# A two-layer decoder trunk in one kernel: one more seven-product pair in four feed-forward blocks, residual additions by accumulating DMAs, and bank sums ordered ahead of a weight subtraction

## The chip, the cores and the metric

The kernel runs on one core of one Trainium2 chip. The metric is the device time of one execution in microseconds (us); the median of several executions is compared. A change of less than 0.2% (5.1 us) is treated as no change.

## The reference

An input x of 256 rows by 2048 features (float32) passes through two layers. Layer 0 mixes with an mLSTM and a Mamba-2 head group between one input and one output projection, layer 1 with block-sparse attention. Each layer ends in a SwiGLU feed-forward stage of width 5632, which is where most of the change lies:

```python
def swiglu(x, w_gate, w_up, w_down):
    return (jax.nn.silu(x @ w_gate) * (x @ w_up)) @ w_down

for layer in range(DEPTH):
    xn = rms_norm(x, norm_mix[layer])
    x = x + (mixer_mlstm_ssd(xn, ...) if layer % 2 == 0 else mixer_moba(xn, ...))
    x = x + swiglu(rms_norm(x, norm_ffn[layer]), *ffn_params[layer])
return rms_norm(x, final_norm)
```

## The kernel before

Every float32 product is made of three matmuls: each operand is split into a high part (rounded to the fast format fp32r) and a low part (the rest), and high x high, high x low and low x high are added up (`add`, L487 to L489). Activations are split once and kept as blocks of four row tiles (class `KT`). Weights are streamed: `weights` loads 256 rows of two strips of 512 columns into the tile `raw` (two DMAs of 512 KB on the SP queue), ScalarE casts them to `wh` (L453) and VectorE subtracts to get `wl` (L455).

`block` computes the product of 256 rows by two strips over `nk` row tiles of the weights. It takes the row tiles in pairs, each pair in one of two ways, given by a plan string such as PSPSPSPP. A "P" pair is done as eight block products of two row tiles: 24 matmuls into the four accumulators `F` (called `acc_f`). An "S" pair is done by Winograd's form of Strassen's scheme with seven block products: 21 matmuls into `F` and four more accumulators `E` (called `acc_e`). For it VectorE forms sums of weight quarters (`sums`: L462, L463, L465) and sums of activations (`activation_sums`, held in a tile called `skh` with three buffers or `skx`). `pairs` says which row-tile pairs are done the S way; `ahead` holds functions that are called at a given place of the plan, here to make activation sums (`sums_of`).

All eight banks of the accumulator memory are in use: `F` in the two double banks, `E` in the four others. After the last S pair the bank sums of `E` are formed in the tile `pre` (L537 to L542; one buffer in the feed-forward stages), and after the last pair `F` is added. A next block begins with a P pair and writes the same double banks, so its first matmul waits until `F` of the block before was read.

The feed-forward stage (`ffn`) works in groups of 4, 4 and 3 strips of 512 hidden columns. For each strip, `hidden` computes gate and up in one block, adds `F` to the sums (`joined`, L1093), applies SiLU and the product (L1096, L1097), and has the result h turned into row tiles for the down projection (for all strips but a group's last, through a copy `hr` made by a DMA on GpSimd's queue, L1100). Then `add_blocks` does the down projection of the group in two halves of 1024 output columns (`q` = 0 and 1), and adds the result to the residual `xr_` (called `xres`) with VectorE: `add_all(F, both)`, then `add_all(pre, joined)`, both L975. In the last group of a layer it also starts the norm of what follows (`finish`, or `whole` at the very end, where parts go by accumulating DMAs, `add_into`, L982).

The order on each engine comes from a scheduler, which takes the instructions by priority (`tc.high_priority` raises it) as they become ready in its own time model; the engines then run them in that order. `tc.issue_after(i)` puts what is issued inside it behind instruction `i` where both are on the same engine. Small pieces of work are queued with `later` and run at ticks between pairs (`tick`), the transposes of x and h among them (`transpose_split`, L282 and L284).

Of the kernel before, what the change touches and what calls it, by code (L numbers as in the profile page):

```python
# [19 lines left out]
NT = T // P  # L20
# [3 lines left out]
STRIP = 512  # L24
# [14 lines left out]
PLAN_X4 = "PSPSSPSP"  # L39
# [3 lines left out]
PLAN_H = {4: ("PSPSPSPP", "PSPSPSPP"), 3: ("PSPSPP", "PSPSPP")}  # L43
PLAN_H_LATE = "PPSPSP"
# [23 lines left out]
def hybrid_trunk(ctx: ExitStack, tc: tile.TileContext, a: dict, out: bass.AP):  # L68
# [205 lines left out]
    def transpose_split(kt, b, src, gcol, half):  # L274

        pt = aux_bank("p_tr")
        for j in range(2):
            for t in range(NT):
                c = (2 * half + j) * P
                to = pt[:, j * T + t * P:j * T + (t + 1) * P]  # L280
                if src[t].dtype == F32R:
                    nc.tensor.transpose(to.bitcast(F32R), src[t][:, c:c + P], ident_r)  # L282
                else:
                    nc.tensor.transpose(to, src[t][:, c:c + P], ident)  # L284
        first = kt.name in ("x1", "x2", "x3") or kt.name[0] == "h" and src[0].dtype == F32
        with tc.high_priority(offset=1200 if first else 0):
            turned(kt, b, pt.rearrange("p (a b) -> p a b", a=2), gcol, half)
# [153 lines left out]
    def weights(src, row, summed):  # L441

        shape = [P, 4, STRIP]
        raw = unit("raw", shape, "raw")
        for i, (w, col) in enumerate(src):
            nc.sync.dma_start(raw[:, 2 * i:2 * i + 2, :],
                              w[row:row + 2 * P, col:col + STRIP].rearrange("(a p) f -> p a f", p=P))

        def parts(of, cuts):
            h = high_unit(4)  # L450
            l = unit("wl", shape, "wl", F32R)
            for c in cuts:
                turn["cast"] = nc.scalar.copy(h[:, c, :], of[:, c, :])  # L453
            for c in cuts:
                turn["sub"] = nc.vector.tensor_sub(l[:, c, :], of[:, c, :], h[:, c, :].bitcast(F32))  # L455
            return h, l

        with tc.high_priority(offset=800):
            if not summed:
                return parts(raw, (slice(0, 2), slice(2, 4)))  # L460
            sums = unit("raw", shape, "sums")
            nc.vector.tensor_sub(sums[:, 0:2, :], raw[:, 2:4, :], raw[:, 3:0:-2, :])  # L462
            nc.vector.tensor_sub(sums[:, 2, :], raw[:, 2, :], sums[:, 1, :])  # L463
            first = parts(raw, (slice(0, 3),))
            nc.vector.tensor_sub(sums[:, 3, :], raw[:, 0, :], sums[:, 2, :])  # L465
            return first + parts(sums, (slice(0, 2), slice(2, 4)))
# [3 lines left out]
    def block(src, kt, row, nk, plan, after_sums=None, lead=1, pairs=None, ahead=(), turns=0):  # L470
# [14 lines left out]
        def add(dst, a, b, start, stop):  # L485
            (ah, al), (bh, bl) = a, b
            nc.tensor.matmul(dst, ah, bh, start=start, stop=False)  # L487
            nc.tensor.matmul(dst, ah, bl, start=False, stop=False)  # L488
            nc.tensor.matmul(dst, al, bh, start=False, stop=stop)  # L489

        first_s, last_s = plan.find("S"), plan.rfind("S")
        joint = "pre" in [tag for _, tags in stage["pools"] for tag in tags] and not turn.get("gains")
# [472 lines left out]
    def add_blocks(w, kt, row, nk, plans, finish=None, begin=None, whole=None, pairs=None, ahead=((), ())):  # L965

        for q in range(2):
            c0 = 2 * q * STRIP
            dst = [xr_[t][:, c0 + n_ * STRIP:c0 + (n_ + 1) * STRIP] for t in range(NT) for n_ in range(2)]

            wide_dst = [xr_[t][:, c0:c0 + 2 * STRIP].rearrange("p (a b) -> p a b", a=2) for t in range(NT)]

            def add_all(what, joined):
                for d, x in zip(dst, what) if joined is None else zip(wide_dst, joined):
                    last = nc.vector.tensor_add(d, d, x)  # L975
                return last

            if begin is not None:
                begin(2 * q)
                begin(2 * q + 1)  # L980
            def add_into(d, x):
                nc.gpsimd.dma_start(d, x, accum_op=OP.add)  # L982

            def add_sums(pre, joined):
                add_into(dst[0], pre[0])
                turn["added"] = nc.vector.tensor_add(dst[1], dst[1], pre[1])
                for i in (2, 3):
                    add_into(dst[i], pre[i])

            final = q and whole is not None  # L990
            if final:
                ahead = ahead[0], tuple((3, finish, s) for s in range(2))
            F, pre, both, joined = block(((w, c0), (w, c0 + STRIP)), kt, row, nk, plans[q], add_sums if final else None,
                                         2 if final else 1, pairs and list(pairs), ahead[q],
                                         2 if q and finish is not None and plans[q] == PLAN_X else 0)
            if final:
                with tc.high_priority(offset=1600):
                    whole(dst, F, turn.pop("added"))
                continue
            if whole is not None:  # L1000
                with tc.high_priority(offset=1600):
                    for i in range(4):
                        nc.vector.tensor_add(pre[i], pre[i], F[i])
                        add_into(dst[i], pre[i])
                continue
            with tc.high_priority(offset=1600):
                added = add_all(F, both)
                if "sums" in turn:
                    with tc.issue_after(added.ins):
                        turn.pop("sums")()  # L1010
            with tc.high_priority(offset=800):
                add_all(pre, joined)
            if finish is not None:
                for s in (2 * q, 2 * q + 1):
                    finish(s)
# [68 lines left out]
    def ffn(xt, r, wg_, wu_, wd, name, finish, begin=None, whole=None):  # L1084

        def hidden(hT, i, s, plan, copied):
# [3 lines left out]
            hs = []  # L1090
            for t in range(NT):
                with tc.high_priority(offset=1600):
                    nc.vector.tensor_add(joined[t], joined[t], both[t])  # L1093
                g, u = pre[2 * t:2 * t + 2]
                h = t2([P, STRIP], "h")
                nc.scalar.activation(h, g, AF.Silu, scale=r[:, t:t + 1])  # L1096
                nc.vector.scalar_tensor_tensor(h, u, r[:, t:t + 1], h, op0=OP.mult, op1=OP.mult)  # L1097
                if copied:
                    hr = t2([P, STRIP], "hr", F32R)
                    nc.gpsimd.dma_start(hr.bitcast(F32), h)  # L1100
                    h = hr
                hs.append(h)
# [3 lines left out]
        for n in (4, 4, 3):  # L1106
            hT = KT(f"h{name}{first}", 4 * n)
            hT.sums = summed(PLAN_H[n][0])
            for i in range(n):
                hidden(hT, i, first + i, PLAN_X4 if i == 1 else PLAN_X if first + i else PLAN_LATE, i < n - 1)  # L1110
            last = first + n == DFF // STRIP
            add_blocks(wd, hT, first * STRIP, 4 * n, (PLAN_H[n][0], PLAN_H_LATE if last and whole is None else PLAN_H[n][1]),
                       *((finish, begin, whole) if last else ()), pairs=list(hT.sums))
            first += n

    open_stage("f", FFN)
# [232 lines left out]
```

## Time and profile before

| What | Value |
|---|---|
| Median of 3 runs | 2541.66 us (2541.06 to 2542.31) |
| Profiled execution | 2541.8 us, span 2540.0 us, granted TensorE clock 0.999 |
| TensorE matmul busy (PE) | 2529.7 us, 12096 matmuls |
| TensorE weight loads (PEld) | 2118.0 us |
| VectorE busy (DVE) | 2229.0 us, 2842 instructions |
| ScalarE busy (ACT) | 1485.7 us |
| GpSimd busy (POOL) | 54.2 us |
| DMA | 507.23 MB, 200 GB/s in the mean |

The profile shows one execution. Rows of a timeline give the start, the length, the engine, the line of the kernel, the operation and out<-in by the names of the tiles; rows grouped by line give the count, the busy time and the mean length in ns, and then the idle time of the engine before them with what ended it. The drawn end of a matmul is modelled and overlaps the next one, so spacing is read from starts. The time of a run is the span of the instructions and about 2 us around it.

### The profile page before, as it was taken

Reading aid. Unit: us, or ns where it says so; the run is one execution under the profiler, and the core shown is the slowest. Engines: PE = TensorE matmul, PEld = TensorE weight load, DVE = VectorE, ACT = ScalarE, POOL = GpSimd, SP = SyncE. Lnnn points to the kernel's source line nnn. Section 1 sums busy time; section 2 is a strip of 40 time slices with the busy share of each in tenths; the row PEclk is TensorE's granted clock in tenths of the full one; section 3 lists DMA queues with packets and bytes.
Section 4 is the critical chain, followed back from the end, with each engine's and each line's share of the span. In section 5 each row is a group of like instructions: output and inputs, shape, how many; then the busy total and the mean of one; then the engine's idle time right before and its main releaser. Section 6 shows DMA issues by size and latency. Waiting matters only on the chain.

```text
span 2540.0 us, 32552 instructions
## 1 busy us (share of the span) xinstructions
PE 2529.7 (100%) x12096; PEld 2118.0 (83%) x12096; DVE 2229.0 (88%) x2842; ACT 1485.7 (58%) x1970; POOL 54.2 (2%) x104
## 2 busy tenths in 40 slices
PE   9999999999999999999999999999999999999998
PEld 8888888888888888888888888888888888888887
DVE  5776788898989999999999997767999999999998
ACT  6465565566656555555455665666565545555555
POOL 1000000000000000000000000000000000000001
PEclk9999999999999999999999999999999999999999
DMA  8665566565665656565656647554556566655666
GB/s 286 178 212 182 167 223 182 174 215 184 195 218 176 223 174 232 191 224 181 225 199 215 199 165 238 166 166 149 199 184 214 194 212 208 212 200 201 222 208 196
DMA packets 257679, 507.23 MB, mean 200 GB/s; under 512 B 16120, under 2 KB 16272, under 8 KB 257008
## 3 DMA queue, kind: packets, MB, share of 16 engines
q1 hardware_dynamic: 250384, 483.99, 58.1%
q0 software_dynamic: 5984, 19.26, 2.2%
q8 instruction: 95, 1.56, 0.2%
q10 hardware_dynamic: 1152, 1.90, 0.2%
q14 instruction: 64, 0.52, 0.1%
HBM read 492.66 MB, written 2.14 MB: 195 GB/s over the span
## 4 chain that ended last, share of the span: by engine, by line
PE 95%; DVE 3%; DMA 1%; issue 1%; ACT 0%; SPq 0%; DVEq 0%; POOLq 0%; POOL 0%; ACTq 0%
PE acc_f L487 18%; PE acc_f L489 18%; PE acc_f L488 18%; PE acc_w L396 12%; PE acc_w L400 6%; PE acc_e L487 4%; PE acc_e L488 4%; PE acc_e L489 4%; PE acc_a L425 2%; PE acc_a L427 2%; PE acc_a L426 2%; DVE wl L455 1%; PE p_tr L284 1%; PE p_y L933 1%; DMA raw<-in_l_ffn_up 0%
## 5 line engine op out<-in xcount | busy, mean ns | idle before, releaser
L453 ACT CAST wh<-raw 128x1024 fp32r<-128x1024 f32 (+1 forms) x562 | 622.0, 1148 | 385.9 <-PE acc_f L489 313.1
L455 DVE TENSOR_TENSOR wl<-raw,wh 128x1024 fp32r<-128x1024 f32 (+1 forms) x562 | 739.4, 1338 | 83.8 <-ACT wh L453 80.2
L487 PE MATMUL acc_f<-wh,x 128*128 128x512 f32 x1080 | 422.5, 391 | 0.5 <-DVE pre L1093 0.5
L453 ACT CAST wh<-sums 128x1024 fp32r<-128x1024 f32 x252 | 258.8, 1052 | 279.9 <-PE acc_f L489 131.0
L489 PE MATMUL acc_f<-wh,x 128*128 128x512 f32 x1080 | 420.6, 389 | 0.0
L488 PE MATMUL acc_f<-wl,x 128*128 128x512 f32 x1080 | 420.4, 389 | 0.0
L381 DVE TENSOR_TENSOR wl<-raw,wh 128x1024 fp32r<-128x1024 f32 x223 | 269.9, 1222 | 122.4 <-ACT wh L380 120.6
L380 ACT CAST wh<-raw 128x1024 fp32r<-128x1024 f32 x223 | 230.8, 1048 | 191.5 <-PE acc_w L396 96.4
L455 DVE TENSOR_TENSOR wl<-sums,wh 128x1024 fp32r<-128x1024 f32 x252 | 300.6, 1218 | 10.5 <-ACT wh L453 10.0
L396 PE MATMUL acc_w<-xa,wh 128*128 128x512 f32 x768 | 265.7, 396 | 0.2 <-DVE xa L227 0.2
L487 PEld LDWEIGHTS acc_f<-wh,x 128*128 128x128 f32 x1080 | 202.7, 188 | 43.3 <-DVE pre L1093 1.9
L489 PEld LDWEIGHTS acc_f<-wh,x 128*128 128x128 f32 x1080 | 202.7, 188 | 42.4
L488 PEld LDWEIGHTS acc_f<-wl,x 128*128 128x128 f32 x1080 | 202.8, 188 | 41.5
L400 PE MATMUL acc_w<-xa,wl 128*128 128x256 f32 x768 | 208.6, 282 | 0.0
L396 PE MATMUL acc_w<-x,wh 128*128 128x512 f32 x512 | 182.5, 399 | 0.4 <-DVE pre L1203 0.4
L396 PEld LDWEIGHTS acc_w<-xa,wh 128*128 128x128 f32 x768 | 144.2, 188 | 31.3 <-ACT wh L373 0.5
L462 DVE TENSOR_TENSOR sums<-raw 128x1024 f32<-128x1024 f32 x126 | 153.4, 1217 | 7.5 <-DMA raw<-in_l_w_qkv 1.9
L400 PE MATMUL acc_w<-x,wl 128*128 128x256 f32 x512 | 143.4, 280 | 0.0
L400 PEld LDWEIGHTS acc_w<-xa,wl 128*128 128x128 f32 x768 | 142.0, 189 | 1.1
L396 PEld LDWEIGHTS acc_w<-x,wh 128*128 128x128 f32 x512 | 96.3, 188 | 21.2 <-DVE pre L1203 0.7
L487 PE MATMUL acc_e<-wh,skx 128*128 128x512 f32 x264 | 102.9, 391 | 0.0
L489 PE MATMUL acc_e<-wh,skx 128*128 128x512 f32 x264 | 102.8, 389 | 0.0
(373 smaller groups left out, 4692.3 us busy)
## 6 DMA issues: line engine op xcount, KB each, us to landing
raw<-in_l_w_in SPq DMA_DIRECT2D x191, 512.0 KB, 3.7
raw<-in_l_ffn_gate SPq DMA_DIRECT2D x176, 512.0 KB, 3.9
raw<-in_l_ffn_up SPq DMA_DIRECT2D x176, 512.0 KB, 4.9
raw<-in_l_ffn_down SPq DMA_DIRECT2D x176, 512.0 KB, 5.0
raw<-in_l_w_qkv SPq DMA_DIRECT2D x96, 512.0 KB, 4.6
raw<-in_l_w_out SPq DMA_DIRECT2D x64, 512.0 KB, 5.1
raw<-in_l_w_o SPq DMA_DIRECT2D x32, 512.0 KB, 4.8
hr<-h POOLq DMA_DIRECT2D x32, 256.0 KB, 3.2
```

The costliest lines, as they stand in the source:

```text
L380: nc.scalar.copy(wh[:, ks, :], raw[:, ks, :])
L381: turn["low"] = nc.vector.tensor_sub(wl[:, ks, :], raw[:, ks, :], wh[:, ks, :].bitcast(F32))
L396: return nc.tensor.matmul(banks[f], wh[:, kk, f * P:(f + 1) * P], kt.both(k0 + kk), start=k0 + kk == 0, stop=False, skip_group_check=True)
L400: nc.tensor.matmul(banks[f][:, :T], wl[:, kk, f * P:(f + 1) * P], kt.parts(k0 + kk)[0], start=False, stop=k0 + kk == nk - 1, skip_group_ch ...
L425: nc.tensor.matmul(banks[t], xh[:, ts], wh[:, kk, :], start=k0 + kk == 0, stop=False)
L426: nc.tensor.matmul(banks[t], xh[:, ts], wl[:, kk, :], start=False, stop=False)
L453: turn["cast"] = nc.scalar.copy(h[:, c, :], of[:, c, :])
L455: turn["sub"] = nc.vector.tensor_sub(l[:, c, :], of[:, c, :], h[:, c, :].bitcast(F32))
L462: nc.vector.tensor_sub(sums[:, 0:2, :], raw[:, 2:4, :], raw[:, 3:0:-2, :])
L487: nc.tensor.matmul(dst, ah, bh, start=start, stop=False)
L488: nc.tensor.matmul(dst, ah, bl, start=False, stop=False)
L489: nc.tensor.matmul(dst, al, bh, start=False, stop=stop)
```

## The change

It has four parts.

1. In `add_blocks` with no `finish` (the two groups of each layer that are not the last, both halves), the bank sums of `F` are added into `pre` (`joined`), and an accumulating DMA on GpSimd's queue adds each row block's 1024 columns to the residual.
2. In the same groups the second half takes the plan PSPSSPSP for PSPSPSPP, with the activation sums of pair 7 made at place 3 of the plan.
3. The first addition of `F` into `joined`, in `hidden` and in `add_blocks`, is remembered as `emptied`, and the next S pair's second weight subtraction (L463) is put behind it on VectorE.
4. Transposes of x whose source is float32 are put behind the third matmul of the product issued last.

```diff
--- before.py
+++ after.py
@@ -280,7 +280,8 @@
                 to = pt[:, j * T + t * P:j * T + (t + 1) * P]
                 if src[t].dtype == F32R:
                     nc.tensor.transpose(to.bitcast(F32R), src[t][:, c:c + P], ident_r)
-                else:
+                    continue
+                with tc.issue_after(turn["product"].ins) if kt.name[0] == "x" else nullcontext():
                     nc.tensor.transpose(to, src[t][:, c:c + P], ident)
         first = kt.name in ("x1", "x2", "x3") or kt.name[0] == "h" and src[0].dtype == F32
         with tc.high_priority(offset=1200 if first else 0):
@@ -460,7 +461,8 @@
                 return parts(raw, (slice(0, 2), slice(2, 4)))
             sums = unit("raw", shape, "sums")
             nc.vector.tensor_sub(sums[:, 0:2, :], raw[:, 2:4, :], raw[:, 3:0:-2, :])
-            nc.vector.tensor_sub(sums[:, 2, :], raw[:, 2, :], sums[:, 1, :])
+            with tc.issue_after(turn.pop("emptied").ins) if "emptied" in turn else nullcontext():
+                nc.vector.tensor_sub(sums[:, 2, :], raw[:, 2, :], sums[:, 1, :])
             first = parts(raw, (slice(0, 3),))
             nc.vector.tensor_sub(sums[:, 3, :], raw[:, 0, :], sums[:, 2, :])
             return first + parts(sums, (slice(0, 2), slice(2, 4)))
@@ -486,7 +488,7 @@
             (ah, al), (bh, bl) = a, b
             nc.tensor.matmul(dst, ah, bh, start=start, stop=False)
             nc.tensor.matmul(dst, ah, bl, start=False, stop=False)
-            nc.tensor.matmul(dst, al, bh, start=False, stop=stop)
+            turn["product"] = nc.tensor.matmul(dst, al, bh, start=False, stop=stop)
 
         first_s, last_s = plan.find("S"), plan.rfind("S")
         joint = "pre" in [tag for _, tags in stage["pools"] for tag in tags] and not turn.get("gains")
@@ -1003,6 +1005,13 @@
                         nc.vector.tensor_add(pre[i], pre[i], F[i])
                         add_into(dst[i], pre[i])
                 continue
+            if finish is None and joined is not None:
+                with tc.high_priority(offset=1600):
+                    for t in range(NT):
+                        emptied = nc.vector.tensor_add(joined[t], joined[t], both[t])
+                        turn.setdefault("emptied", emptied)
+                        add_into(wide_dst[t], joined[t])
+                continue
             with tc.high_priority(offset=1600):
                 added = add_all(F, both)
                 if "sums" in turn:
@@ -1090,7 +1099,7 @@
             hs = []
             for t in range(NT):
                 with tc.high_priority(offset=1600):
-                    nc.vector.tensor_add(joined[t], joined[t], both[t])
+                    turn.setdefault("emptied", nc.vector.tensor_add(joined[t], joined[t], both[t]))
                 g, u = pre[2 * t:2 * t + 2]
                 h = t2([P, STRIP], "h")
                 nc.scalar.activation(h, g, AF.Silu, scale=r[:, t:t + 1])
@@ -1109,8 +1118,12 @@
             for i in range(n):
                 hidden(hT, i, first + i, PLAN_X4 if i == 1 else PLAN_X if first + i else PLAN_LATE, i < n - 1)
             last = first + n == DFF // STRIP
-            add_blocks(wd, hT, first * STRIP, 4 * n, (PLAN_H[n][0], PLAN_H_LATE if last and whole is None else PLAN_H[n][1]),
-                       *((finish, begin, whole) if last else ()), pairs=list(hT.sums))
+            if last:
+                add_blocks(wd, hT, first * STRIP, 4 * n, (PLAN_H[n][0], PLAN_H_LATE if whole is None else PLAN_H[n][1]),
+                           finish, begin, whole, pairs=list(hT.sums))
+            else:
+                add_blocks(wd, hT, first * STRIP, 4 * n, (PLAN_H[n][0], PLAN_X4), pairs=[*hT.sums, 7],
+                           ahead=((), ((3, sums_of, hT, 7, False),)))
             first += n
 
     open_stage("f", FFN)
```

## The prediction

> **What bounds the kernel now.** I read the busy times first, then the forty slices, then the waits of TensorE alone, and last the timelines around the block changes that the diff touches.
>
> ```profile
> PE 2529.7 (100%) x12096; PEld 2118.0 (83%) x12096; DVE 2229.0 (88%) x2842; ACT 1485.7 (58%) x1970; POOL 54.2 (2%) x104
> DVE 5776788898989999999999997767999999999998
> POOL 1000000000000000000000000000000000000001
> ```
>
> TensorE (PE) is busy for 2529.7 of 2540.0 us, so the time is its instruction count times their spacing, plus few stalls. VectorE (DVE) is the second engine: 9 tenths or more in nearly every slice of both feed-forward stages. Whatever adds VectorE work there must be weighed. GpSimd (POOL), which issues the new DMAs, is nearly idle.
>
> The spacing is read from starts, since the drawn length of a matmul (0.39 us) overlaps the next one.
>
> ```profile
> 959.78 0.39 PE L487 MATMUL acc_e<-wh,ha 128*128 128x512 f32 x1
> ...
> 972.48 0.39 PE L489 MATMUL acc_f<-wh,ha 128*128 128x512 f32 x1
> ```
>
> These are the first and last of 57 matmuls in a row: 12.70 us / 56 = 0.227 us each.
>
> TensorE's own waits, from the list of waits of its weight loads (us in total, times, longest):
>
> ```profile
> PEld acc_f L487 <- DVE pre L1093: 1.9, 6, 0.8
> PEld p_tr L284 <- DVE xres L975: 0.4, 2, 0.3
> ```
>
> The first row is what the bank-sum part of the change can aim at: six waits, 1.9 us in all, for the VectorE addition at L1093 that empties the accumulator banks acc_f of the block before.
>
> **The change part by part.**
>
> *Products.* A pair of row tiles costs 24 matmuls as eight products (P: 4 outputs x 2 tiles x 3) and 21 as seven (S: 7 x 3). The second half of a down-projection group goes from PSPSPSPP (three S) to PSPSSPSP (four S), in the two groups of each layer that are not the last: four blocks, 4 x 3 = 12 matmuls fewer, 12 x 0.227 = **-2.72 us**. TensorE has no idle time there, so all of it lies on the path. The Trainium skill, "TensorE: Matmul & The Clock Gate", section "Back-to-back issue gap", gives a sustained roofline of about 131 ns for a matmul of 512 columns, by which this term would be an estimated -1.6 us; the trace has 227 ns, and the trace decides.
>
> *VectorE's price of that.* The rows, grouped by line in the hidden block at 1057.0 to 1098.5, which already runs PSPSSPSP with the same extra sum:
>
> ```profile
> L455 DVE TENSOR_TENSOR wl<-raw,wh 128x1024 fp32r<-128x1024 f32 x8 | 9.5, 1219 | 1.2 <-ACT wh L453 1.2
> L455 DVE TENSOR_TENSOR wl<-sums,wh 128x1024 fp32r<-128x1024 f32 x8 | 9.5, 1218 | 0.0
> L455 DVE TENSOR_TENSOR wl<-raw,wh 128x1536 fp32r<-128x1536 f32 x3 | 5.3, 1754 | 0.0
> L462 DVE TENSOR_TENSOR sums<-raw 128x1024 f32<-128x1024 f32 x4 | 4.9, 1219 | 0.0
> L465 DVE TENSOR_TENSOR sums<-raw,sums 128x512 f32<-128x512 f32 x4 | 2.8, 688 | 0.1
> L463 DVE TENSOR_TENSOR sums<-raw,sums 128x512 f32<-128x512 f32 x4 | 2.7, 684 | 0.0
> L1093 DVE TENSOR_TENSOR pre<-pre,acc_f 128x1024 f32<-128x1024 f32 x2 | 2.4, 1213 | 0.0
> L331 DVE TENSOR_TENSOR xg<-x 128x512 f32<-128x512 f32 x1 | 0.7, 687 | 0.0
> L225 DVE TENSOR_TENSOR skh<-sf,skh 128x512 fp32r<-128x512 f32 x1 | 0.7, 683 | 0.0
> L317 DVE TENSOR_TENSOR sf<-sf,xg 128x128 f32<-128x128 f32 x1 | 0.3, 285 | 0.0
> ```
>
> An S unit is 1.22 + 0.68 + 0.69 + 1.75 + 2 x 1.22 = 6.78 us of VectorE, a P unit 2 x 1.22 = 2.44: +4.34. The activation sums of pair 7 are 0.69 + 4 x 0.285 + 0.68 = +2.51. The residual additions go from four of about 1.21 (two over banks, two over pre) to two of the L1093 kind: -2.43. Net +4.4 us in each of the four second halves, -2.43 in the four first halves. The block's stretch before, and the hidden block as a standard (columns: stretch, its length, then PE, PEld, DVE, ACT, POOL busy):
>
> ```profile
> 974.10:1015.50 41.40, 41.40 (x184) 34.30 (x183) 37.58 (x36) 21.07 (x20) 0.00 (x0) 1.00 0.60 203
> 1057.00:1098.50 41.50, 41.50 (x190) 34.40 (x188) 40.27 (x44) 24.11 (x24) 1.08 (x2) 1.00 0.58 199
> ```
>
> 37.58 + 4.4 = 42.0 us of rows against 41.40 - 0.68 = 40.7 us of TensorE. Rows of neighbouring VectorE instructions overlap by about 0.08 us (see the starts below: 1.22 long, next one 1.13 later); eight more instructions take 0.6 off, which leaves 41.4. So the block is over its budget by 0.7 (1.3 without that correction). What covers it: the weight splits run ahead of TensorE, the hidden block at 40.27 of 41.50 keeps TensorE busy throughout, and the half before the new one is relieved of 2.43 us. I take 0; the bounds are 0 and 4 x 1.3 = +5.2. ScalarE gains 2 to 3 us of casts on 21 of 41: hidden. The weight loads on SP stay the same in number and size.
>
> *Bank sums ahead of a weight subtraction.* Two of the block changes that end in PSPSSPSP now, VectorE and TensorE:
>
> ```profile
> 843.78 1.21 DVE L542 TENSOR_TENSOR pre<-pre,acc_e 128x1024 f32<-128x1024 f32 x1
> 844.92 0.68 DVE L463 TENSOR_TENSOR sums<-raw,sums 128x512 f32<-128x512 f32 x1
> 845.52 2.34 DVE L1093 TENSOR_TENSOR pre<-pre,acc_f 128x1024 f32<-128x1024 f32 x2
> 845.79 0.46 PE L487 MATMUL acc_e<-wh,x 128*128 128x512 f32 x1
> 846.79 0.50 PE L487 MATMUL acc_f<-wh,x 128*128 128x512 f32 x1 [0.54 <-DVE pre L1093]
> ...
> 1095.83 1.21 DVE L542 TENSOR_TENSOR pre<-pre,acc_e 128x1024 f32<-128x1024 f32 x1
> 1096.96 0.68 DVE L463 TENSOR_TENSOR sums<-raw,sums 128x512 f32<-128x512 f32 x1
> 1097.57 2.34 DVE L1093 TENSOR_TENSOR pre<-pre,acc_f 128x1024 f32<-128x1024 f32 x2
> 1098.46 0.46 PE L487 MATMUL acc_e<-wh,x 128*128 128x512 f32 x1
> 1098.83 0.50 PE L487 MATMUL acc_f<-wh,x 128*128 128x512 f32 x1
> ```
>
> The weight subtraction L463 stands between the last bank sum of acc_e (L542) and the first of acc_f. With it behind, L1093 starts 845.52 - 844.92 = 0.60 us earlier. The long wait of the six (0.8) loses 0.60 of it; its rest stays, since L542 itself is late there. The other five share 1.9 - 0.8 = 1.1 us, 0.22 each, less than 0.60, so they go: **-1.7 us**, bounds 0 and -1.9. Queued behind the moved L463 are L465, the casts of sums on ScalarE and the splits for the later products of the next S unit; they come one bank sum (1.1 us) later. That unit is second in its block, a P unit of 24 x 0.227 = 5.4 us ahead of it, so no TensorE wait from this.
>
> Four new changes of the same shape arise (second halves that now end in S then P). With the order fixed I take 0; bound 4 x 0.22 = +0.9.
>
> *The swap where nothing waited.* At the six changes from a hidden block to a down projection, L463 now runs in time that would else be idle:
>
> ```profile
> 1178.75 1.76 DVE L455 TENSOR_TENSOR wl<-raw,wh 128x1536 fp32r<-128x1536 f32 x1
> 1180.43 0.68 DVE L463 TENSOR_TENSOR sums<-raw,sums 128x512 f32<-128x512 f32 x1
> 1181.03 1.21 DVE L1093 TENSOR_TENSOR pre<-pre,acc_f 128x1024 f32<-128x1024 f32 x1
> ...
> 1180.30 0.39 PE L489 MATMUL acc_f<-wh,x 128*128 128x512 f32 x1
> ```
>
> The second bank's last matmul starts at 1180.30 and is drawn to 1180.69. VectorE is free at 1180.43; if nothing else fills the place, it idles 1180.69 - 1180.43 = 0.26 us, and the down projection behind it is short of VectorE. Bounds 0 and 6 x 0.26 = +1.6; another ready instruction may fill the gap, so I take a third, **+0.5**.
>
> *Residual additions by DMA.* Sixteen DMAs of 512 KB (eight halves, two row blocks) come in on POOL's queue. The nearest rows are the seven accumulating DMAs of 256 KB at the end of the kernel (L982) and the refill of the tile pre:
>
> ```profile
> L982 POOL DMA_DIRECT2D xres<-pre x7: 839/848/1182, 2498.8 to 2525.5; - x7
> DMA to landing us min/median/max: 3.1/5.8/7.9
> 974.89 1.22 DVE L975 TENSOR_TENSOR xres<-xres,acc_f 128x1024 f32<-128x1024 f32 x1
> 1002.14 0.59 ACT L537 COPY pre<-acc_e 128x512 f32<-128x512 f32 x1
> ```
>
> About 0.85 us of POOL each, POOL else idle; next on its queue is the next hidden block's copy of h, tens of us later. There is one buffer of pre: the copy L537 of the next block must wait for the landing. The last bank sum ends at 976.1 and L537 comes at 1002.14, 26 us later, against landings of 3.1 to 7.9 (twice that for twice the size is 16). I take 0. Their 8.4 MB run beside the weight loads; at 200 GB/s they would lengthen a load by a few us that is issued well ahead: 0, bound +0.5.
>
> *Transposes of x held behind the last product.* They keep their number. Between -0.4 (the wait for xres quoted above) and +0.4 for the reverse; I take 0.
>
> **Sum**: -2.72 - 1.7 + 0.5 = -3.9. The profiled execution took 2541.8 us (span 2540.0 and 1.8 around it); 2541.8 - 3.9 = 2537.9. The median of the runs is 0.14 lower, so **2537.8**, -0.15%. I call 0.2%, 5.1 us, the bound of what counts as a change.
>
> **Rivals.**
>
> *More than the sum.* All 1.9 us go, the swap costs nothing, the x transposes give 0.4, and the relief of 2.43 us in each first half takes out small delays that no row names, perhaps 1: -6.0, 2535.6. For it: VectorE is the only engine that TensorE waits for here. Against: the rows name hardly more than 1.9. Chance 0.17.
>
> *Only the products count.* Another VectorE instruction takes the place of L463, or L542 is what is late; the four new changes wait 0.22 each and the swap costs 0.5: -2.72 + 0.9 + 0.5 = -1.3, 2540.4. Against it: 0.60 is well over 0.22. Chance 0.14.
>
> *Slower: VectorE over budget in the second halves.* Place: the fourth S unit of each new PSPSSPSP block. Each us that VectorE is over and the splits' lead does not cover comes back as a wait of TensorE; from 3.9 / 4 = 0.98 us a block the change loses. At the upper 1.3 us: -3.9 + 5.2 = +1.3, 2543.0. For it: 42.0 against 40.7. Against: the hidden block at 40.27 of 41.50. Chance 0.08, a quarter of it beyond +0.2%.
>
> *The accumulating DMAs hold pre.* At a landing past 26 us, L537 waits, with the casts behind it, in the next block each time; five times the 5.8 us median is 29, 3 us x 8 = +24, -3.9 + 24 = +20, 2561.7. Against: 7.9 is the longest here, under a VectorE as busy. Chance 0.03. The Trainium skill, "SBUF — State Buffer", section "SBUF: two separate sides", warns of a DMA issued from GpSimd that starves while VectorE holds the shared port, 620 ns becoming 3100; the landings of L982 beside it bear that out little.
>
> **How the numbers follow.** Forecast (-2 to -5 us, 2536.7 to 2539.7): 0.58. Faster by over 0.2%: 0.17, the first rival. Slower: 0.03 + 0.02 = 0.05. Within: 0.78. The range takes in the large gain, the products alone and part of the overload: 2535.3 to 2541.4.
>
> **What would show it.** 12 matmuls fewer (12084); no wait of acc_f for L1093 above 0.2 us but one; L463 behind the first bank sum at each change; the second halves 0.68 us shorter; L975 left only in the other stages and the last groups, and sixteen DMAs pre to xres that land within 16 us. Wrong if TensorE waits for wl inside the new blocks, if L537 waits for a DMA, or if the down projections' first halves grow by more than 0.3 us.

## The result and the profile after

The changed kernel takes 2556.79 us (median of 6 runs, 2555.82 to 2558.87) against 2542.21 us (2541.06 to 2542.72) for the kernel before in the same runs: a ratio of 1.0059, 95% interval 1.0046 to 1.0072. It is 14.6 us slower. The forecast was 2537.8 us with a range up to 2541.4: wrong in sign and outside the range.

The page of the changed kernel, span and busy times:

```profile
span 2554.0 us, 32619 instructions
PE 2532.4 (99%) x12084; PEld 2116.8 (83%) x12084; DVE 2235.5 (88%) x2866; ACT 1492.2 (58%) x1978; POOL 69.5 (3%) x120
```

Twelve matmuls fewer, and yet the span is 14.0 us longer. (PE's busy time rose by 2.7 us with fewer matmuls: matmuls at a lower clock, below, add some 3.3 us; what else adds to it is not divided here.) The waits of TensorE, in us in total, times, longest, name new ones:

```profile
PE acc_f L489 <- ACT wh L454: 5.1, 1, 5.1
PE acc_e L490 <- DVE wl L456: 3.4, 5, 1.0
PE acc_f L490 <- DVE wl L456: 1.4, 1, 1.4
...
PE acc_f L489 <- DVE pre L1102: 1.0, 6, 0.2
```

To find where the time went I cut both traces at the first matmul of every block and compared the lengths. Five stretches of before, then the same five of after (columns: stretch, its length, busy PE, PEld, DVE, ACT, POOL, granted clock, DMA share, GB/s). They are a second half of a down projection, the hidden block behind it, the block behind a hidden PSPSSPSP block, the second half of the output projection of layer 1, and the first feed-forward block of layer 1:

```profile
974.06:1015.54 41.48, 41.48 (x184) 34.35 (x183) 37.66 (x36) 21.07 (x20) 0.00 (x0) 1.00 0.60 203
1015.54:1057.02 41.48, 41.48 (x184) 34.35 (x183) 37.63 (x36) 21.91 (x21) 0.00 (x0) 1.00 0.61 203
1098.46:1140.99 42.53, 42.53 (x193) 35.00 (x193) 41.80 (x46) 25.53 (x29) 1.07 (x2) 1.00 0.65 227
1792.92:1836.19 43.27, 43.27 (x200) 36.06 (x200) 41.39 (x52) 28.83 (x40) 0.00 (x0) 1.00 0.62 202
1836.19:1880.30 44.11, 44.11 (x204) 36.53 (x203) 42.85 (x58) 27.58 (x39) 0.69 (x1) 1.00 0.61 212
```

```profile
973.23:1014.03 40.80, 40.80 (x182) 33.80 (x180) 36.92 (x36) 23.18 (x22) 1.45 (x2) 1.00 0.69 207
1014.03:1057.05 43.02, 42.02 (x184) 34.21 (x183) 38.74 (x37) 21.79 (x21) 1.68 (x2) 1.00 0.77 243
1098.48:1141.39 42.91, 42.75 (x195) 34.99 (x193) 41.81 (x47) 25.54 (x29) 1.07 (x2) 1.00 0.65 226
1794.18:1842.69 48.51, 43.43 (x200) 35.88 (x199) 44.50 (x61) 30.83 (x45) 0.00 (x0) 0.98 0.65 220
1842.69:1891.63 48.94, 47.52 (x203) 38.73 (x204) 40.06 (x49) 25.26 (x35) 1.12 (x1) 0.92 0.45 151
```

Done for all blocks, the account is this (us, after less before):

| Place | Each | Sum |
|---|---|---|
| four second halves that got an S pair | -0.68 | -2.7 |
| four hidden blocks behind them (the new changes) | +1.55, +1.22, +1.08, +1.29 | +5.1 |
| six blocks behind hidden PSPSSPSP blocks (the old changes) | +0.30 to +0.37 | +2.1 |
| end of layer 1's output projection, first feed-forward block | +5.23, +4.83 | +10.1 |
| four first halves | -0.05 to -0.20 | -0.4 |
| last block | +0.72 | +0.7 |
| the rest, mostly ahead of the first block | | -0.8 |
| sum, the difference of the spans | | +14.0 |

Two stretches also differ between profiled executions of kernels that do the same work there, over all the runs below by -0.8 to +1.7 us (ahead of the first block) and -0.5 to +1.7 us (the attention of layer 1). So the blocks are compared one by one; spans and medians do not follow from them to the tenth.

The first row is the forecast to the hundredth. The next three are where it broke, and each has its rows.

**The ten us.** TensorE's last products of the output projection and the first of the next stage, with the SP queue's load and ScalarE's cast between them (timeline of after: start, length, engine, line):

```profile
1836.23 0.47 SPq L447 DMA_DIRECT2D raw<-in_l_ffn_gate  x1
...
1841.59 1.04 ACT L454 CAST wh<-raw 128x1024 fp32r<-128x1024 f32 x1
...
1837.22 0.39 PE L491 MATMUL acc_f<-wh,o 128*128 128x512 f32 x1
1842.69 1.22 PE L489 MATMUL acc_f<-wh,x 128*128 128x512 f32 x2 [5.08 <-ACT wh L454]
1845.33 0.79 PE L490 MATMUL acc_f<-wl,x 128*128 128x512 f32 x1 [1.42 <-DVE wl L456]
1845.92 0.63 PE L491 MATMUL acc_f<-wh,x 128*128 128x512 f32 x1
1846.35 0.63 PE L489 MATMUL acc_f<-wh,x 128*128 128x512 f32 x1
```

The load is issued at 1836.23 and takes 5.3 us to land, which is when the cast starts. TensorE stands still for 5.08 us for the high parts of the stage's first weights, then 1.42 us for their low parts. And afterwards it is slow: starts 0.43 us apart (1846.35 - 1845.92) where 0.227 is normal. The granted clock (the column behind POOL's) says why:

```profile
1837.60:1840.70 3.10, 0.01 (x1) 0.00 (x0) 3.10 (x8) 2.61 (x3) 0.00 (x0) 1.00 1.05 402
1840.80:1850.90 10.10, 6.79 (x15) 4.91 (x16) 10.10 (x16) 4.99 (x11) 0.19 (x1) 0.50 0.24 73
1851.10:1855.00 3.90, 3.90 (x23) 3.31 (x22) 0.38 (x2) 1.72 (x2) 0.72 (x1) 1.00 0.56 215
```

Those first weights are late because of the tile they are loaded into, by the code of `unit`, which the diff does not touch:

```python
if kind == "raw" and stage["spare"]:
    turn["spare"] = turn.get("spare", -1) + 1
    if turn["spare"] % 4 == 3:
        return held_tile("rawx", shape, name, dt)
```

Every fourth tile of kind `raw` comes from a fourth buffer, `rawx`, which belongs to the feed-forward stage's own pool; by the code, its place is one that the attention stage's tiles hold before, which the output projection reads. The load that the first cast waits for is the last of five that the SP queue issues for the stage up to there, right behind one issued at 1835.30. In the kernel before, a load goes out fifth likewise (1835.10), but there, by the count, `rawx` holds the third pair. (Why the scheduler puts the load of `rawx` fifth, no run shows.) An S pair takes two such tiles (`raw` and `sums`), a P pair one. The two new S pairs of layer 0 move the counter on by two, so that `rawx` falls to the first pair of the stage instead of the third. That is the theory that the first two experiments test.

**The block changes.** First an old change (VectorE, then TensorE), the one whose rows before stand last in that part of the prediction:

```profile
1095.86 1.21 DVE L544 TENSOR_TENSOR pre<-pre,acc_e 128x1024 f32<-128x1024 f32 x1
1096.99 1.75 DVE L456 TENSOR_TENSOR wl<-raw,wh 128x1536 fp32r<-128x1536 f32 x1
1098.66 2.34 DVE L1102 TENSOR_TENSOR pre<-pre,acc_f 128x1024 f32<-128x1024 f32 x2
1100.93 0.68 DVE L465 TENSOR_TENSOR sums<-raw,sums 128x512 f32<-128x512 f32 x1
...
1097.86 0.79 PE L282 MATMUL p_tr<-ident_r,hr 128*128 128x128 f32 x8
...
1099.93 0.51 PE L489 MATMUL acc_f<-wh,x 128*128 128x512 f32 x1 [0.16 <-DVE pre L1102]
```

The weight subtraction (now L465) does stand behind the bank sums. But in the place it left stands the wide split of the same S pair, 1.75 us instead of 0.68. The bank sums start 1.67 us after this place comes free (1098.66 less 1096.99), where L463 had kept them 0.61 us (1097.57 less 1096.96). And a new change:

```profile
1012.48 1.21 DVE L544 TENSOR_TENSOR pre<-pre,acc_e 128x1024 f32<-128x1024 f32 x1
1013.62 1.75 DVE L456 TENSOR_TENSOR wl<-raw,wh 128x1536 fp32r<-128x1536 f32 x1
1015.28 2.34 DVE L1011 TENSOR_TENSOR pre<-pre,acc_f 128x1024 f32<-128x1024 f32 x2
...
1014.03 0.39 PE L489 MATMUL acc_e<-wh,x 128*128 128x512 f32 x1
1015.42 0.50 PE L490 MATMUL acc_e<-wl,x 128*128 128x512 f32 x1 [1.00 <-DVE wl L456]
```

The same order on VectorE, and here TensorE has nothing else to do: at the old change eight transposes (0.79 us) lie between the blocks. Counted from the start of the next block, the last sum of acc_e starts 2.62 us ahead at the old change (1098.48 less 1095.86) and 1.55 us ahead here (1014.03 less 1012.48). At both, TensorE's queue has products of the S pair, into acc_e, ahead of the P pair's, and these need the wide split's low part: no wait there, 1.00 us here.

### The profile page after: what moved, and what is told of

It reads as the page before. It is cut to its first block, busy times and chain, and to the rows that moved or that the text cites. A ratio compares the mean times of both kernels' runs of the same rounds, so it can differ in the third digit from the quotient of the medians.

```text
span 2554.0 us, 32619 instructions
## 1 busy us (share of the span) xinstructions
PE 2532.4 (99%) x12084; PEld 2116.8 (83%) x12084; DVE 2235.5 (88%) x2866; ACT 1492.2 (58%) x1978; POOL 69.5 (3%) x120
## 4 chain that ended last, share of the span: by engine, by line
PE 95%; DVE 3%; issue 1%; DMA 0%; ACT 0%; SPq 0%; DVEq 0%; POOLq 0%; POOL 0%; ACTq 0%
PE acc_f L489 18%; PE acc_f L490 18%; PE acc_f L491 18%; PE acc_w L397 11%; PE acc_w L401 6%; PE acc_e L490 4%; PE acc_e L491 4%; PE acc_e L489 4%; PE acc_a L426 2%; PE acc_a L428 2%; PE acc_a L427 2%; DVE wl L456 1%; PE p_tr L285 1%; PE p_y L935 1%; PE p_num L798 0%
## 5 line engine op out<-in xcount | busy, mean ns | idle before, releaser
L454 ACT CAST wh<-sums 128x1024 fp32r<-128x1024 f32 x260 | 267.2, 1052 | 271.4 <-PE acc_f L491 129.8
L456 DVE TENSOR_TENSOR wl<-sums,wh 128x1024 fp32r<-128x1024 f32 x260 | 311.2, 1218 | 5.2 <-ACT wh L454 4.9
L463 DVE TENSOR_TENSOR sums<-raw 128x1024 f32<-128x1024 f32 x130 | 158.4, 1218 | 19.9 <-DMA raw<-in_l_ffn_up 8.6
L490 PE MATMUL acc_e<-wl,skx 128*128 128x512 f32 x264 | 102.9, 390 | 0.0
L491 PE MATMUL acc_e<-wh,skx 128*128 128x512 f32 x264 | 102.8, 390 | 0.0
```

What stands on the lines that cost most here:

```text
L491: turn["product"] = nc.tensor.matmul(dst, al, bh, start=False, stop=stop)
```

## Experiments

Each is told with the median of the kernel before in the same runs: 2541.55 us (28 runs) beside the first four, 2542.24 (17) beside the next four, 2542.14 (21) beside the last two; the run of part 4 alone has its own.

### The counter alone, in the kernel before

```diff
     open_stage("g", FFN)
+    turn["spare"] += 2
```

> The kernel before with one number changed: at the start of the second feed-forward stage the counter that gives every fourth weight tile to the spare buffer rawx is advanced by 2, as two more S pairs in the first feed-forward stage advance it. Theory A (the spare buffer's turn): the first weight tile of that stage now falls on rawx, whose place is free only when TensorE has done the attention's output projection; its load is issued late, TensorE waits at the block change near 1836 us as it does in the changed kernel (output projection and first hidden block 5.2 and 4.8 us longer), and the run takes about 10 us more, 2552. Rival B (the reordered transposes of x, part 4 of the change, make that stall): no change, 2542.

Measured: 2548.42 us (7 runs), ratio 1.0026 (1.0014 to 1.0037). One line that adds and removes no instruction and changes which tile is used costs 6.9 us, where theory A expected about 10. The waits of TensorE, the cast of the first weights, the two stretches around the stage change, and the clock:

```profile
PE p_tr L284 <- DVE xres L975: 4.4, 2, 3.5
...
PE acc_f L487 <- ACT wh L453: 0.7, 1, 0.7
...
1841.89 1.04 ACT L453 CAST wh<-raw 128x1024 fp32r<-128x1024 f32 x1 [0.96 <-DMA raw<-in_l_ffn_gate]
```

```profile
1793.45:1842.99 49.54, 44.52 (x205) 36.42 (x204) 45.39 (x62) 31.14 (x45) 0.00 (x0) 0.98 0.63 215
1842.99:1888.78 45.79, 45.79 (x199) 38.16 (x199) 39.44 (x47) 25.14 (x35) 1.12 (x1) 0.95 0.47 161
...
1840.80:1847.40 6.60, 5.10 (x18) 4.23 (x19) 5.79 (x9) 5.48 (x14) 0.00 (x0) 0.50 0.12 46
```

The two stretches grow by 6.27 and 1.69 us; every other block stays within 0.1 us of before, except one of the first group (-0.33 us, as in most of the other runs). The wait is put down to x transposes here, since without part 4 these stand in the gap; the first product waits for its weights all the same, whose cast waits for the load, and starts only at 1842.99. The theory of the counter holds; the transposes are not the cause. (One thing in theory A is too strong: the load goes out at 1835.47, before the last product of the output projection, which starts at 1836.47, so it need not wait for all of it.) The first feed-forward block loses 3.1 us less than in the changed kernel: transposes fill the second wait, and the clock is full again from 1847.60 at the latest, where the changed kernel has half until 1850.90.

### The changed kernel with the counter set back

```diff
     open_stage("g", FFN)
+    turn["spare"] += -2
```

> The changed kernel with the same counter set back by 2 at the start of the second feed-forward stage. Theory A: the stall between the attention's output projection and the first hidden block goes, about 10 us less than the changed kernel, 2546.7; what is left over the kernel before (+4.5) are the ten block changes behind PSPSSPSP. Rival B (transposes of x): the stall stays, 2556.8.

Measured: 2548.07 us (10 runs), 1.0026 (1.0017 to 1.0035). Its stretches at a new change, an old change and the stage change:

```profile
1014.89:1057.64 42.75, 42.00 (x185) 34.19 (x183) 38.49 (x37) 21.79 (x21) 1.68 (x2) 1.00 0.76 243
1099.08:1141.97 42.89, 42.73 (x193) 34.95 (x193) 41.77 (x47) 25.51 (x29) 1.07 (x2) 1.00 0.64 224
1796.04:1839.32 43.28, 43.28 (x201) 36.05 (x200) 41.51 (x52) 28.76 (x40) 0.00 (x0) 1.00 0.61 203
```

43.28 against 43.27 before, and the first feed-forward block behind it is back as well (-0.09): all 10 us at the stage change are gone, with parts 1 to 4 in place. The losses at the block changes stay: +1.27, +1.15, +1.21, +1.09 at the new ones, about +0.33 at five of the six old ones (the first: -0.33), +0.63 in the last block. What remains of the loss, 6.5 us in the medians, is a matter of the other parts.

### The same without part 3

```diff
-            with tc.issue_after(turn.pop("emptied").ins) if "emptied" in turn else nullcontext():
-                nc.vector.tensor_sub(sums[:, 2, :], raw[:, 2, :], sums[:, 1, :])
+            nc.vector.tensor_sub(sums[:, 2, :], raw[:, 2, :], sums[:, 1, :])
```

> As the last kernel, and the weight subtraction is not put behind the bank sum (part 3 of the change undone). Theory C (with the short subtraction behind the bank sum, the wide weight split of 1.75 us takes the place ahead of it): the six old block changes behind PSPSSPSP go back to the lengths of the kernel before (0.34 us less each), the four new ones lose most of the 1.1 to 1.5 us that they are longer by; together 5 to 6 us less than the last kernel, about 2541. Rival D (the longer changes come from the bank sums having to wait for the sums of acc_e, as pre takes the place of the residual): the four new changes stay 1 us or more longer, about 2545.

Measured: 2543.91 us (10 runs), 1.0009 (1.0000 to 1.0018). The old changes return to before within 0.03 us each and the last block to +0.01: their loss was part 3's. The new changes still cost +0.91, +1.81, +1.46 and +0.92. So the order of L463 is not the main cause there. The first new change:

```profile
1013.58 0.68 DVE L464 TENSOR_TENSOR sums<-raw,sums 128x512 f32<-128x512 f32 x1
1014.18 2.34 DVE L1010 TENSOR_TENSOR pre<-pre,acc_f 128x1024 f32<-128x1024 f32 x2
...
1015.45 0.50 PE L488 MATMUL acc_f<-wh,x 128*128 128x512 f32 x1 [0.62 <-DVE pre L1010]
```

With the short instruction in the place the first product still waits for its bank. Ahead of that stands the last sum of acc_e, which ends only at 1013.66 (start 1012.45, 1.21 long): the last S pair stands last but one in the block.

### The wide split also behind the bank sum

Part 3 with the split moved too, at the block changes behind PSPSSPSP, so that nothing of the next S pair's weights stands ahead of the bank sum:

```diff
...
+            with tc.issue_after(emptied.ins) if emptied and turn["plan"] == PLAN_X4 else nullcontext():
+                first = parts(raw, (slice(0, 3),))
```

> The changed kernel with the counter set back, and behind a block that ended in PSPSSPSP the wide weight split of the next S pair is put behind the first bank sum too, not only the short subtraction. Theory C: the bank sums come right behind the sums of acc_e, the waits at all ten changes go, also the 0.22 us that the kernel before had; 2546.7 less 4 x 1.3, 6 x 0.34 and 6 x 0.25 is about 2538. Rival D: the changes stay longer than in the kernel before, 2544 or more, or the late split makes TensorE wait in the S pair instead.

Measured: 2541.03 us (10 runs), 0.9999 (0.9990 to 1.0009), 7 us less than with the counter alone set back, and 3 us above the 2538 of theory C. VectorE at the new change:

```profile
1011.58 1.21 DVE L546 TENSOR_TENSOR pre<-pre,acc_e 128x1024 f32<-128x1024 f32 x1
1012.89 2.35 DVE L1014 TENSOR_TENSOR pre<-pre,acc_f 128x1024 f32<-128x1024 f32 x2
1015.16 0.68 DVE L466 TENSOR_TENSOR sums<-raw,sums 128x512 f32<-128x512 f32 x1
1015.77 1.75 DVE L456 TENSOR_TENSOR wl<-raw,wh 128x1536 fp32r<-128x1536 f32 x1
```

Now nothing stands between. The old changes gain (-0.89, -0.15, -0.19, -0.18, -0.23, -0.19, in all -1.8), the new ones cost +0.51, +1.08, +0.51, +0.51. These 2.6 us are nearly all that the matmuls saved (2.7).

### The S pairs earlier in the second halves

PSSPSSPP for PSPSSPSP, so that two P pairs stand behind the last S pair, on top of the last experiment.

```diff
+PLAN_H4 = "PSSPSSPP"
...
-add_blocks(wd, hT, first * STRIP, 4 * n, (PLAN_H[n][0], PLAN_X4), pairs=[*hT.sums, 7],
+add_blocks(wd, hT, first * STRIP, 4 * n, (PLAN_H[n][0], PLAN_H4), pairs=[*hT.sums, 7],
```

> The kernel with counter set back and the wide split behind the bank sum, and in the four second halves the plan PSSPSSPP in place of PSPSSPSP: the same number of S pairs, two P pairs behind the last. Theory D (behind an S, P end the bank sums of acc_f, which now add into pre, come late because the sums of acc_e are late): the four block changes lose their 0.5 to 1.1 us, the halves stay 40.80 long, about 2.6 us less in sum, 2538.4. Rival F (two S pairs side by side early in the block starve TensorE of splits): the halves grow by 1 us or more each and eat it up, 2542.

Measured: 2549.03 us (7 runs), 1.0028 (1.0017 to 1.0039). The second half and the block behind it:

```profile
972.66:1015.77 43.11, 41.38 (x181) 33.59 (x180) 39.00 (x38) 23.37 (x22) 1.46 (x2) 1.00 0.78 243
1015.77:1057.26 41.49, 41.49 (x184) 34.37 (x184) 36.33 (x35) 21.71 (x21) 1.68 (x2) 1.00 0.72 228
```

The new changes are free (+0.01 to +0.02 us): with the last S pair, and so the last sums of acc_e, earlier, the banks are read in time. But the halves themselves take 43.11 instead of 40.80 us: with the S pairs crowded, TensorE waits for their low parts (6.7 us in 8 waits in all). The cure costs 2.3 us a half and saves 0.5 to 1.1 at its change.

### Each part alone

Part 2 alone (the plan with the four S pairs and the sums of pair 7, counter set back):

> Part 2 alone: the kernel before with PSPSSPSP in the four second halves, its residual additions on VectorE as before, no reordering, and the counter of the spare buffer set back by 2. Theory D: added to the residual, the bank sums of acc_f need not wait for the sums of acc_e, so the four new block changes cost 0 to 0.3 us and the whole gains 2 to 2.7 us, 2539. Rival C (the order of the weight work alone makes the new changes late): they are 0.9 us or more longer here too, as in the kernel with no reordering, 2542 or more.

Measured: 2543.28 us (11 runs, one of them 3148.23), 1.0005 (0.9996 to 1.0014). The halves are 0.68 us shorter, the blocks behind them 0.59 to 0.66 longer, the next ones 0.25 to 0.29, and four of the old changes 0.32 to 0.36, with part 3 absent. At those four TensorE waits for a cast on ScalarE that a product of the S pair needs (four waits in `PE acc_e L487 <- ACT wh L453`, 1.0 us in all). The products save 2.7 us and nothing is left of it.

Part 3 alone:

> Part 3 alone, at the block changes behind hidden blocks. Theory C: each of the six changes behind PSPSSPSP grows by 0.3 to 0.4 us, for the wide split takes the freed place, +2 us in all, and the down projections' first halves stay within 0.1 us. Rival (the forecast): the six lose 0.2 us or more each.

Measured: 2545.39 us, one run. The old changes +0.34, +0.34, +0.34, +0.49 and +0.35, only the first -0.15; two of the six first halves of down projections +0.79 and +0.37, where at most 0.1 was expected. (The place of the +0.49 has +0.48 and +0.47 in the runs of part 1 and part 4 alone too, so that one is not clearly part 3's.) Part 3, as it is ordered, costs 2.4 to 2.9 us in these blocks; the further 1.7 us of this profile lie ahead of the first block.

Part 1 alone:

> Part 1 alone: residual additions of the four groups by sixteen accumulating DMAs, plans and order as before. Forecast: nothing is waiting for them, every block keeps its length within 0.1 us, and they land within 16 us. Rival: weight loads are slowed or the tile pre is held, and the blocks behind the down projections grow by 0.3 us or more each.

Measured: 2540.81 us, one run. The blocks behind the down projections are within 0.01 us of before. One hidden block is longer by 0.48 us, against the expected 0.1: VectorE waits there 0.40 us for a weight load (`[0.40 <-DMA raw<-in_l_ffn_up]`, at 2165.28). The run of part 4 alone, which has no such DMAs, shows the same wait and +0.47 at the same place. The rows of the accumulating DMAs (16 of them the new ones):

```profile
L982 POOL DMA_DIRECT2D xres<-pre x23: 835/847/1181, 972.6 to 2524.5; - x23
DMA to landing us min/median/max: 3.1/5.3/8.4
```

Part 4 alone:

> Part 4 alone (the float32 transposes of x put behind the last product's third matmul), with none of the other parts. Theory G: it only moves transposes that stand in a wait to where the wait is, so the starts of the blocks after the output projections (first feed-forward blocks of both layers) and everything else stay within 0.2 us of before: 2541 to 2543 us. Rival: kept behind a product, the transposes come late for the casts of x that the next stage's first product needs; then the first block after each stage change starts 0.4 us or more later, at three stage changes +1.2 us or more, 2543 to 2544 us, and a wait of TensorE for x would be listed.

Measured: 2542.23 us, beside 2542.66 for the kernel before, one run each. The first feed-forward blocks start as before (+0.01 and -0.07 us in the lengths); no new wait for x. Apart from the late load just told of, no gain or loss of it shows.

### The correct order alone, in the kernel before

Both the subtraction and the wide split behind the bank sum, only at the changes behind hidden PSPSSPSP blocks:

```diff
...
+            late = emptied and turn["plan"] == PLAN_X4
+            with tc.issue_after(emptied.ins) if late else nullcontext():
+                nc.vector.tensor_sub(sums[:, 2, :], raw[:, 2, :], sums[:, 1, :])
+                first = parts(raw, (slice(0, 3),))
```

> The kernel before with only this: behind a block that ended in PSPSSPSP, the wide split and the short subtraction of the next S pair stand behind the first bank sum. Theory C: the six changes lose 0.15 to 0.25 us each and the first of them 0.9, nothing else moves; about -1.9 us. Rival: the split, now later, makes TensorE wait in the S pair; no gain.

Measured: 2542.15 us (11 runs), 0.9999 (0.9990 to 1.0008). The six old changes: -0.82, -0.18, -0.18, -0.16, -0.23, -0.17, in all -1.7 us. (The first of them is 0.06 to 0.24 us shorter also in three runs that change nothing there, so the edit's share of the 0.82 is smaller.) In the profile the last group's first half in each layer (+0.43 and +0.33) and one hidden block (+0.54) take 1.3 us back; what they leave, 0.4 us, is within the interval of the medians.

### What the runs point to

The S pairs without the DMAs, the residual on VectorE, the first bank sum ahead of the last sums of acc_e, subtraction and split behind it, counter set back:

```diff
-                            if plan == PLAN_H_LATE:
+                            if plan == PLAN_H_LATE or turn.get("defer"):
...
+                        if turn.pop("defer", False):
+                            with tc.issue_after(last.ins):
+                                turn.pop("sums")()
```

> A version meant to keep the gain: PSPSSPSP in the four second halves, counter set back, the residual additions on VectorE as before, the first of them (over acc_f) ahead of the last sums of acc_e in those halves, and behind PSPSSPSP the wide split and the short subtraction behind the first bank sum. Theory D: added to the residual, the bank sum need not wait for acc_e, so the four new block changes cost 0 to 0.2 us, the halves stay 40.80 and the six old changes lose 0.2 us each and one 0.9: -2.7 - 1.9 = about -4.6 against the kernel before, 2537. Rival: VectorE has no time left for the seventh product's weights in the second halves, the waits move into the block behind them, and the gain is under 1.5 us.

Measured: 2540.24 us (11 runs), 0.9992 (0.9984 to 1.0001). VectorE at the new change:

```profile
1012.06 1.22 DVE L980 TENSOR_TENSOR xres<-xres,acc_f 128x1024 f32<-128x1024 f32 x1
1013.19 1.22 DVE L546 TENSOR_TENSOR pre<-pre,acc_e 128x1024 f32<-128x1024 f32 x1
1014.32 1.22 DVE L980 TENSOR_TENSOR xres<-xres,acc_f 128x1024 f32<-128x1024 f32 x1
```

The first bank is read ahead of the last sum of acc_e. That is possible only because the residual, not `pre`, takes the banks: with the bank sums added into `pre`, as in part 1, they must follow the sums of acc_e. The new changes cost +0.25, +0.21, +0.21, +0.21 and the blocks behind them +0.25 each, which theory D had not reckoned with. It is 1.9 us faster in the median, not 4.6, and its interval just takes in no change: the lowest of all versions, not a proven gain.

## Why the prediction was wrong, point by point

**Products, -2.72.** Right: the four halves are 0.66 to 0.68 us shorter in every version with the plan PSPSSPSP.

**VectorE's price in the second halves, 0.** Right for the halves themselves: no wait inside them. But the forecast looked for the price inside the block, and it lies at the block's end and in the blocks behind (part 2 alone: +2.55 at the changes, +1.1 in the blocks after next, +1.4 at the four old changes behind those).

**"The weight loads on SP stay the same in number and size."** They do, and that was the failed step that cost most: 10.1 of the 14.0 us between the two profiles. Number and size were weighed and the place they land in was not. The new S pairs of layer 0 take two more tiles, which moves the turn of `rawx` in the next stage by two. Shown from both sides: the shift alone in the kernel before costs 8.0 us in those two stretches, setting it back in the changed kernel takes 10.1 off (8.7 in the medians). The 2 us between the two go with the x transposes, which in the kernel before run in the gap and after it, and with the clock, which is full again some 3.5 us earlier there. No rival had this mechanism.

**"The weight subtraction L463 stands between the last bank sum of acc_e and the first of acc_f. With it behind, L1093 starts 0.60 us earlier": -1.7.** The wait was real and the size was about right: with nothing in between, the six changes gain 1.7 us (the order alone), if a little of the first one's 0.82 is not its own. The step failed on what fills the place: the scheduler put the 1.75 us split there, so they lost 2.1 us. The rival "only the products count" named this, "another VectorE instruction takes the place of L463", but priced it at no gain; a longer instruction in the place is a loss.

**"With the order fixed I take 0; bound 4 x 0.22 = +0.9" for the new changes.** Failed, 5.1 us. The rows of 0.22 came from changes where eight transposes of 0.79 us lie between the blocks; nothing lies there at the new ones. Without the order (part 3 left out) they cost as much, 5.1; with the full order 2.6; with the first bank read into the residual ahead of the last sum of acc_e, 0.9. That points to how late the banks are read. How the sum divides between the missing transposes, the late sums of acc_e and the queue order of TensorE was not measured apart; only that earlier S pairs take all of it away at this place.

**The swap before the down projections, +0.5.** The first halves behind them came out 0.05 to 0.20 us shorter in four cases and at most 0.07 longer in the last groups. A loss does appear in two of the six with the full order alone (+0.43 and +0.33) and in two with part 3 alone (+0.79 and +0.37, one run).

**Residual DMAs, 0.** Right: alone they leave the blocks behind the down projections within 0.01 us, and the landings are 3.1 to 8.4 us against the 26 us until L537 needs the tile. The rival that they hold `pre` did not come.

**Transposes of x, 0.** Right.

## What to carry to other kernels

Putting one instruction behind another frees a place in an in-order queue; look up which ready instruction of the same engine is next and how long it is, and move that one too, or the wait grows. A buffer that is handed out by a running count carries the effect of a small edit into stages far from it: when a change adds a tile, work out which later tile gets which buffer, above all across a change of stage. And what an added product costs on the second engine is to be sought at the end of its block, where the accumulators must be emptied, as well as inside it.

## What the runs showed of the hardware

A TensorE wait can cost more than its length. The last product ahead of the gap of 5.08 us is drawn to 1837.61 (1837.22 and 0.39). The granted clock is 1.00 until 1840.70 and 0.50 from 1840.80 to 1850.90, and matmuls start 0.43 us apart instead of 0.227. Of the 4.83 us that the first feed-forward block lost, 1.42 are the second wait; most of the rest is this: 5.3 us at half speed from 1845.3 hold what 2.8 us do at full speed, and the two matmuls ahead of that wait take 1.22 us for what is otherwise 0.45 (2 x 0.227). The Trainium skill, "TensorE: Matmul & The Clock Gate", section "What's actually happening", states the same: half the clock after an idle window of about 3.4 us, full again after about as much sustained work, in a window that runs freely. The trace agrees on the half, and the clock fell 3.1 to 3.2 us behind the drawn end; back to full took 5 to 6 us of work here (from 1845.33). The whole stretch at half lasts 10.1 to 10.4 us here (the gaps between the rows above are the bounds), and 6.6 to 7.0 us with the counter moved in the kernel before: about three times and two times the 3.4 us that the Trainium skill gives. The waits of 1.0 us at the block changes show no such drop (clock 1.00 in their stretches).
